# Last product in two token quarters with their own norms, conv pages from the common pool, residual updates two pages later

## The chip, the cores and the metric

The kernel runs on one core of one Trainium2 chip. The metric is the device time of one execution in microseconds (us); lower is better. A core has TensorE (matrix products; PE in the rows, its weight loads PEld), VectorE (DVE), ScalarE (ACT), GpSimd (POOL) and SyncE (SP), which here issues every DMA. TensorE writes into PSUM only; a PSUM bank holds 128x512 float32 values.

## What is computed

One layer of a hybrid backbone on 1024 latent tokens with 1024 channels, on a 16 x 64 grid: a modulated norm, a recurrent and a Fourier head group, an output projection with a gated residual; then the gated MLP with a 3x3 depthwise convolution, a gated residual and a last RMS norm. The change touches only the part from the convolution on:

```python
def conv_ffn(h, w_up, w_dw, b_dw, w_down, rows, cols):
    a, u = jnp.split(h @ w_up, 2, axis=-1)             # 1024 -> 2 x 2816
    a = depthwise_conv_3x3(a.reshape(B, rows, cols, D_FF), w_dw)
    a = a.reshape(B, L, D_FF) + b_dw
    return (jax.nn.gelu(a) * u) @ w_down               # 2816 -> 1024
...
h2 = modulate(rms_norm(x, norm2[l]), sh2, sc2)
x = x + gt2 * conv_ffn(h2, w_up[l], w_dw[l], b_dw[l], w_down[l], rows, GRID_W)
...
return rms_norm(x, norm_f)
```

## The kernel before

**Arithmetic.** All data are float32. For each product both operands are split into a high part (rounded, a copy on ScalarE, L62) and a low part (the rest, a subtraction on VectorE, L63); three TensorE products (high x high, high x low, low x high) are then summed in PSUM. Channels lie on the partitions and tokens along the free axis, so a tile is 128 channels x 512 tokens (one half of the tokens) or 128 x 1024 (a "page").

**MLP up (`norm2`, `ffn`, `product` L859, `plain` L74).** The 2816 hidden channels are 22 tiles `ff` of 128. The first two (`PLAIN`, ff 0 and 1) are computed by plain products, the other 20 by seven products of half size (a scheme of the Strassen kind, with sums U1 to U4 of blocks of the input as operands, made on VectorE at L808 to L819 in pages of the tag `cv`). For each ff the running sums are copied out of PSUM by ScalarE ("snap", L939) before TensorE goes on adding into the same bank.

**`gated`.** For each ff the gate branch `pa` lies in PSUM (tag `g`, two slots). ScalarE writes the centre tap and the bias into a page `cv` (L922); VectorE adds the eight other taps (L930); ScalarE applies the gelu (L932); VectorE multiplies by `u` (L933); then the page is stored to DRAM (`gd<-cv`). The tag `cv` has two slots, so a third page waits until the store of an earlier one has landed.

**MLP down (`down`).** The last product, 2816 to 1024, is done by seven products of half size again, q1, r5, r6, q3, q7, q2, q4 in this order, into the accumulators X (four banks of the tag `m`) and Z (two double banks of the tag `g`). A product has 6 "pages" p = 0 to 5; a page holds two blocks of 128 hidden channels, the last one a single block. For each page `prep` loads or adds up the weight side and the token side, `operands` splits both (L62, L63), and `step` (L1036) issues, for each of 4 output tiles j, three matmuls of 128 x 512 per block: 24 matmuls a page, 132 a product. The split pages come from three pairs of tags in turn (`wh`/`wl` twice, then `pg`; `ws`, `sh`/`sl`, `sh`/`sl`), each with two slots. The last two pages are held back and run tile by tile (`tail`), so that accumulator j is complete before j+1.

After each product `update` (L1067, VectorE) adds the accumulator times the gate to the residual x of one (token half, channel half); the first update of each loads x from DRAM (`pg<-x1d`). Token half 1 is complete after q7; `final` (L1158 on) norms, transposes and stores it inside q4, at its page 2, along with `squares` (sum of squares and transposes of x[0,0], L1107 to L1120). After q4 `update(0, 1, X)` and `last` finish token half 0: squares and norm gain (L1129, L1130), sums over channels by products with ones (L1135), 16 transposes (L1120), `rsqrt_mean` (L87 to L92), eight scalings out of PSUM on VectorE and ScalarE (L1147, L1149) and eight stores of 128 x 512.

**What sets the order.** A planner places the instructions: it steps through a model of the machine with modelled durations, and gives each engine the ready instruction that stands first in the program (blocks under `high_priority` go ahead). Slots of a tag are handed out in the same run. On the chip each engine then works through its own list strictly in order, and SP its DMAs too: what waits at the head holds up all behind it.

Of the kernel before, what the change touches and what calls it, by code (L numbers as in the profile page):

```python
# [34 lines left out]
class Kern:  # L35
# [389 lines left out]
    def hgrn(self, h, g):  # L425
# [60 lines left out]
        for d in range(2):  # L486
            s = st[d]
            f = g[d][0]
            c0, c1 = (0, 1) if d == 0 else (1, 0)
            A, Z = self.sm(16, f"A{d}"), self.sm(16, f"Z{d}")  # L490
            ZA, AZ = self.sm(8, f"ZA{d}"), self.sm(8, f"AZ{d}")
# [362 lines left out]
    def product(self, out, w, name, first):  # L854
        B = self.B[name]
        for kt in range(4):
            q, t = slice(kt * P, (kt + 1) * P), slice((kt % 2) * 512, (kt % 2 + 1) * 512)
            for j, (a, b) in enumerate(((0, 0), (0, 1), (1, 0))):
                self.nc.tensor.matmul(out, w[a][:, q], B[kt // 2][b][:, t], start=(first and kt == 0 and j == 0),  # L859
                                      stop=(kt == 3 and j == 2), skip_group_check=not first)  # L860
# [13 lines left out]
    def ffn(self):  # L874
# [9 lines left out]
        for ff in range(PLAIN, NF):  # L884
# [10 lines left out]
            with first():  # L895
                sv = snap(X)
            Z = self.pst("m")
            self.product(Z, w["S1"], "U1", True)
            with first():
                s5 = snap(Z)  # L900
            self.product(X, w["S3"], "U3", False)
# [15 lines left out]

    def gated(self, ff, pa, u):
        nc, V, v = self.nc, self.nc.vector, self.vec
        cv = self.pg(F32, "cv")  # L920
        w9 = lambda t: v[:, V_WDW + ff * 9 + t:V_WDW + ff * 9 + t + 1]
        nc.scalar.activation(cv, pa, AF.Identity, bias=v[:, V_BDW + ff:V_BDW + ff + 1], scale=w9(4))  # L922
        a3, c3 = pa.rearrange("p (r c) -> p r c", c=64), cv.rearrange("p (r c) -> p r c", c=64)
        for dr in (-1, 0, 1):
            for dc in (-1, 0, 1):
                if dr == 0 and dc == 0:
                    continue
                ro, co = slice(max(0, -dr), 16 - max(0, dr)), slice(max(0, -dc), 64 - max(0, dc))
                ri, ci = slice(max(0, dr), 16 + min(0, dr)), slice(max(0, dc), 64 + min(0, dc))
                V.scalar_tensor_tensor(c3[:, ro, co], a3[:, ri, ci], w9((dr + 1) * 3 + dc + 1), c3[:, ro, co],  # L930
                                       op0=MUL, op1=ADD)
        nc.scalar.activation(cv, cv, AF.Gelu_apprx_tanh)  # L932
        V.tensor_tensor(cv, cv, u, op=MUL)  # L933
        g = self.tile([P, 1024], F32, "gd")
        self.load(g, cv)
        self.gd.append(g)
# [6 lines left out]
    def down(self):  # L943
# [3 lines left out]
        nc, V, wd = self.nc, self.nc.vector, self.I["wd"]  # L947
        ng = self.sm(8, "ng2")
# [75 lines left out]
                out.append((hi, lo))  # L1024
            return out

        def product(pts, prep, first, then=None):

            n = (NF // 2 + 1) // 2

            def step(p, W, G, j):
                for i in range(num(p)):
                    w = slice(i * 512 + j * P, i * 512 + (j + 1) * P)
                    t = slice(i * 512, (i + 1) * 512)
                    for m, (a, b) in enumerate(((0, 0), (0, 1), (1, 0))):
                        nc.tensor.matmul(pts[j], W[a][:, w], G[b][:, t], start=first and p == 0 and i == 0 and m == 0,  # L1036
                                         stop=p == n - 1 and m == 2, skip_group_check=not first)

            tail = []
            for p in range(n):  # L1040
                if p == 2 and then:
                    then()
                W, G = operands(*prep(p), p)
                if p < n - 2:
                    for j in range(4):
                        step(p, W, G, j)
                else:
                    tail.append((p, W, G))
            for j in range(4):
                for t in tail:  # L1050
                    step(*t, j)

        x = {}

        def residual(half, r):
            x[half, r] = []
            for i in range(2):
                t = self.pg()
                self.load(t, self.x1d[half, 2 * r + i])
                x[half, r] += [t[:, :512], t[:, 512:]]  # L1060

        def update(half, r, pts):
            if (half, r) not in x:
                residual(half, r)
            for j in range(4):
                g = (ng if r else self.gt2)[:, 4 * r + j:4 * r + j + 1]
                V.scalar_tensor_tensor(x[half, r][j], pts[j], g, x[half, r][j], op0=MUL, op1=ADD)  # L1067

        def wide():
            pp = [self.pst("g"), self.pst("g")]  # L1070
            return [pp[i // 2][:, (i % 2) * 512:(i % 2 + 1) * 512] for i in range(4)]

        X = [self.pst("m") for _ in range(4)]
        product(X, q1, True)
        update(0, 0, X)
        Z = wide()
        product(Z, r5, True)
        update(1, 1, Z)
        product(X, r6, False)
        update(1, 0, X)  # L1080
        product(Z, q3, False)
        update(1, 0, Z)
        del Z
        product(X, q7, False)
        update(1, 1, X)
        Z = wide()
        product(Z, q2, True)
        update(0, 0, Z)
        del Z

        def then():
            residual(0, 1)
            self.final(x.pop((1, 0)) + x.pop((1, 1)))
            self.squares(x[0, 0])

        product(X, q4, False, then)
        update(0, 1, X)
        X.clear()
        self.last(x[0, 0], x[0, 1])

    def squares(self, xs):

        nc, V = self.nc, self.nc.vector
        self.acc = self.pg()
        for d, x in enumerate(xs):
            sq = self.acc[:, :512] if d == 0 else self.tile([P, 512], F32, "sn")
            nc.scalar.activation(sq, x, AF.Square)  # L1107
            if d:
                V.tensor_tensor(self.acc[:, :512], self.acc[:, :512], sq, op=ADD)
            nc.scalar.activation(x, x, AF.Copy, scale=self.vec[:, V_NF + d:V_NF + d + 1])  # L1110
        self.turn = []
        for i in range(4):
            if i % 2 == 0:
                pt = self.pst("g")
            self.turned(pt[:, (i % 2) * 512:(i % 2 + 1) * 512], xs, i)

    def turned(self, pt, xs, i):

        for j in range(4):
            self.nc.tensor.transpose(pt[:, j * P:(j + 1) * P], xs[j][:, i * P:(i + 1) * P], self.ident)  # L1120
        self.turn.append(pt)

    def last(self, xa, xb):

        nc, V = self.nc, self.nc.vector
        parts = [self.acc]
        for j, x in enumerate(xb):
            sq = self.tile([P, 512], F32, "sn")
            nc.scalar.activation(sq, x, AF.Square)  # L1129
            V.tensor_scalar(x, x, self.vec[:, V_NF + 4 + j:V_NF + 5 + j], None, op0=MUL)  # L1130
            parts.append(sq)
        ss = self.pst("m")
        for k, a in enumerate(parts):
            for i in range(4):
                nc.tensor.matmul(ss[:, i:i + 1], a[:, i * P:(i + 1) * P], self.ones[:, 0:1], start=(k == 0 and i == 0),  # L1135
                                 stop=k == 4, skip_group_check=True)
        for i in range(3):
            self.turned(self.pst("m"), xb, i)
        r = self.rsqrt_mean(ss[:, :4], 4, 1.0 / D, "nf")
        del ss  # L1140
        self.turned(self.pst("m"), xb, 3)
        for i in range(4):
            ob = self.pg()
            for h in range(2):
                o, pt = ob[:, h * 512:(h + 1) * 512], self.turn[4 * h + i]
                if h:
                    V.tensor_scalar(o, pt, r[:, i:i + 1], None, op0=MUL)  # L1147
                else:
                    nc.scalar.activation(o, pt, AF.Copy, scale=r[:, i:i + 1])  # L1149
                self.load(self.out[i, :, h * 512:(h + 1) * 512], o)  # L1150

    def final(self, xs):

# [47 lines left out]
NA, WARM, PLAIN = 3, 6, 2  # L1201
# [99 lines left out]
```

## Time and profile before

| | us |
|---|---|
| median of three runs | 1234.57 (1233.62 to 1239.16) |
| the profiled execution, device time | 1235.95 |
| its span, first to last instruction | 1234.2 |
| TensorE busy in the span | 1191.5 (97%) |
| VectorE busy | 913.7 (74%) |
| ScalarE busy | 559.3 (45%) |
| TensorE's mean granted clock | 0.987 of full speed |

Lines of a timeline begin with the start and the busy time in us; a bracket at the end is the engine's idle time just before and what ended it. The rows of a view by stage give busy time and instruction count of each engine, then the granted TensorE clock. Matmuls overlap in their pipeline, so the distance between two starts, not the busy time of one, is what a matmul costs.

### The profile page before, as it was taken

The page shows a single profiled execution, that of the slowest core. Times are in us where ns is not written, and L with a number is a line of the kernel's source. Part 1 is how long each engine was busy: PE and PEld are TensorE (multiplying, and loading weights), DVE is VectorE, ACT ScalarE, POOL GpSimd, SP SyncE. Part 2 cuts the span into 40 slices and gives each one's busy share as a digit, 9 for nine tenths or more (in the row PEclk, how much of TensorE's full clock was granted, in tenths as well). Part 3 has the DMA queues.
Part 4 walks back from the last instruction along what each step waited for, and adds up shares of the span by engine and source line. Part 5 has one row for each costly group of instructions (what it writes and reads, how often), then busy time and mean ns, then how long its engine had stood idle before and what let it go on. Part 6 is the DMA issues. An engine that isn't in the chain of part 4 may idle for free.

```text
span 1234.2 us, 15757 instructions
## 1 busy us (share of the span) xinstructions
PE 1191.5 (97%) x6120; PEld 996.5 (81%) x6120; DVE 913.7 (74%) x1173; ACT 559.3 (45%) x804; POOL 201.7 (16%) x124
## 2 busy tenths in 40 slices
PE   7999999999999999999989999999999999999997
PEld 4688888888998888888868888888888887887876
DVE  5761758585877457577989897888888888997683
ACT  5634545454431424364544444444354433335551
POOL 0000000000000000001336455364463400000000
PEclk9999999999999999999989999999999999999998
DMA  8631101010256037453122322222212438635642
GB/s 327 234 121 38 39 18 35 18 35 18 86 162 205 10 120 263 156 187 103 34 77 77 112 94 78 89 90 86 86 69 94 145 111 304 244 112 185 221 157 99
DMA packets 57867, 146.23 MB, mean 118 GB/s; under 512 B 5568, under 2 KB 5824, under 8 KB 57792
## 3 DMA queue, kind: packets, MB, share of 16 engines
q1 hardware_dynamic: 57792, 145.22, 34.1%
q8 instruction: 48, 0.79, 0.3%
q14 instruction: 27, 0.22, 0.1%
HBM read 125.27 MB, written 19.92 MB: 118 GB/s over the span
## 4 chain that ended last, share of the span: by engine, by line
PE 63%; DVE 14%; ACT 9%; DMA 8%; issue 5%; SPq 0%; POOL 0%; DVEq 0%; ACTq 0%; POOLq 0%
PE psm L859 27%; PE psm L74 16%; PE psg L74 14%; PE psm L1036 3%; DMA wr<-in_wd_dram 2%; DVE cv L930 2%; DVE wl L63 2%; DMA wm<-in_wm_dram 2%; DVE pg L451 1%; DMA pg<-gd 1%; ACT wh L62 1%; DMA wx<-gd 1%; ACT sq L568 1%; DVE sl L63 1%; PE psg L1036 1%
## 5 line engine op out<-in xcount | busy, mean ns | idle before, releaser
L930 DVE SCALAR_TENSOR_TENSOR cv<-psg,vec,cv 128x945 f32<-128x945 f32 (+2 forms) x176 | 213.8, 1219 | 26.9 <-ACT cv L922 23.1
L859 PE MATMUL psm<-pg,sh 128*128 128x512 f32 x640 | 199.1, 393 | 5.5 <-ACT sn L939 5.5
L62 ACT CAST wh<-wr 128x1024 fp32r<-128x1024 f32 x78 | 82.0, 1053 | 144.3 <-PE psg L74 39.7
L859 PEld LDWEIGHTS psm<-pg,sh 128*128 128x128 f32 x640 | 121.3, 190 | 31.6 <-ACT sn L939 6.3
L74 PE MATMUL psg<-pg,wh 128*128 128x512 f32 x472 | 134.8, 394 | 0.0
L63 DVE TENSOR_TENSOR wl<-wr,wh 128x1024 fp32r<-128x1024 f32 x78 | 96.5, 1238 | 41.2 <-ACT wh L62 40.8
L839 POOL TENSOR_TENSOR ws<-wx 128x512 f32<-128x512 f32 x20 | 27.9, 1394 | 601.8 <-DMA wx<-in_wup_dram 568.0
L859 PE MATMUL psm<-pg,sl 128*128 128x512 f32 x320 | 125.4, 392 | 0.0
L74 PEld LDWEIGHTS psg<-pg,wh 128*128 128x128 f32 x472 | 87.2, 188 | 16.8
L74 PE MATMUL psg<-wh,pg 128*128 128x256 f32 x512 | 99.0, 292 | 1.0 <-ACT wh L62 0.8
L859 PE MATMUL psm<-pg,wh 128*128 128x512 f32 x320 | 98.4, 389 | 0.0
L939 ACT ACTIVATE sn<-psm 128x512 f32<-128x512 f32 x80 | 47.6, 596 | 108.7 <-PE psm L859 108.7
L74 PEld LDWEIGHTS psg<-wh,pg 128*128 128x128 f32 x512 | 83.0, 197 | 1.6 <-ACT wh L62 1.4
L74 PE MATMUL psg<-pg,wl 128*128 128x512 f32 x236 | 79.1, 395 | 0.0
L74 PE MATMUL psg<-wl,pg 128*128 128x256 f32 x256 | 74.5, 292 | 4.6 <-DVE wl L63 4.6
L859 PEld LDWEIGHTS psm<-pg,sl 128*128 128x128 f32 x320 | 60.6, 190 | 12.7
L859 PEld LDWEIGHTS psm<-pg,wh 128*128 128x128 f32 x320 | 60.1, 188 | 12.4
L905 POOL TENSOR_TENSOR uu<-sn,sn 128x512 f32<-128x512 f32 x20 | 38.5, 1924 | 183.0 <-ACT sn L939 183.0
L859 PE MATMUL psm<-pg,wl 128*128 128x512 f32 x160 | 62.2, 389 | 0.0
L74 PE MATMUL psm<-pg,pg 128*128 128x128 f32 (+2 forms) x256 | 56.6, 348 | 5.0 <-DVE pg L506 4.7
L221 DVE SCALAR_TENSOR_TENSOR ma<-wm,silu_c,ma 128x512 f32<-128x512 f32 x56 | 41.9, 749 | 17.8 <-DMA wm<-in_wm_dram 17.2
L847 POOL TENSOR_TENSOR sl<-ws,sh 128x1024 fp32r<-128x1024 f32 x20 | 54.1, 2706 | 5.6 <-ACT sh L846 5.5
(368 smaller groups left out, 2590.3 us busy)
## 6 DMA issues: line engine op xcount, KB each, us to landing
wr<-in_wd_dram SPq DMA_DIRECT2D x35, 512.0 KB, 3.7
wm<-in_wm_dram SPq DMA_DIRECT2D x64, 256.0 KB, 3.0
wx<-in_wup_dram SPq DMA_DIRECT2D x22, 512.0 KB, 4.5
wr<-in_wup_dram SPq DMA_DIRECT2D x22, 512.0 KB, 3.6
gd<-cv SPq DMA_DIRECT2D x22, 512.0 KB, 2.6
pg<-gd SPq DMA_DIRECT2D x33, 256.0 KB, 4.9
ld<-in_wm_dram SPq DMA_DIRECT2D x16, 512.0 KB, 7.9
wr<-in_wo_dram SPq DMA_DIRECT2D x16, 512.0 KB, 3.6
```

What stands on the lines that cost most here:

```text
L62: self.nc.scalar.copy(hi, raw)
L63: self.nc.vector.tensor_tensor(lo, raw, hi.bitcast(F32), op=SUB)
L74: self.nc.tensor.matmul(out, lhsT, rhs, start=start, stop=stop)
L221: nc.vector.scalar_tensor_tensor(acc, w, s, acc, op0=MUL, op1=ADD)
L451: V.tensor_tensor_scan(flip(lf, d), flip(lf, d), self.mscan, 0.0, op0=ADD, op1=MUL)
L839: G.tensor_tensor(s31[:, hi], u[:, lo], u[:, hi], op=ADD)
L847: G.tensor_tensor(S31[1], s31, S31[0].bitcast(F32), op=SUB)
L859: self.nc.tensor.matmul(out, w[a][:, q], B[kt // 2][b][:, t], start=(first and kt == 0 and j == 0), stop=(kt == 3 and j == 2), skip_group_ ...
L905: self.nc.gpsimd.tensor_tensor(u[:, h1], s7, s5, op=SUB)
L930: V.scalar_tensor_tensor(c3[:, ro, co], a3[:, ri, ci], w9((dr + 1) * 3 + dc + 1), c3[:, ro, co], op0=MUL, op1=ADD)
L939: self.nc.scalar.mul(dst, src, c)
L1036: nc.tensor.matmul(pts[j], W[a][:, w], G[b][:, t], start=first and p == 0 and i == 0 and m == 0, stop=p == n - 1 and m == 2, skip_group_ch ...
```

## The change

1. **Conv pages.** In `gated` the page of ff 0 and 1 comes from the common pool `pg` (33 pages) in place of the tag `cv`.
2. **Residual updates.** The `update` of a product no longer stands behind it, but inside the next product, ahead of its page 2 (`then`), along with the load of x where it is the first. The order of the products and their accumulators stays; the second use of Z is called Y.
3. **Last product.** In q4 the last three pages are held back, not two. They run first for tokens 0 to 255 of the half (all four j), then for tokens 256 to 511: 120 matmuls of 256 columns in place of 60 of 512. Behind each quarter stands its own `quarter`: update of 128 x 256, squares, sums with ones, `rsqrt_mean` of two columns, scaling, stores. The 16 transposes of x[0,0] move from `squares` into the quarters (the second quarter's eight are put ahead of its update).

```diff
     def gated(self, ff, pa, u):
-        cv = self.pg(F32, "cv")
+        cv = self.pg(F32, "pg" if ff < PLAIN else "cv")
...
-        def product(pts, prep, first, then=None):
+        def product(pts, prep, first, then=None, half=None):
...
-            def step(p, W, G, j):
+            def step(p, W, G, j, q):
...
-                        nc.tensor.matmul(pts[j], W[a][:, w], G[b][:, t], start=first and p == 0 and i == 0 and m == 0,
+                        nc.tensor.matmul(pts[j][:, q], W[a][:, w], G[b][:, i * 512 + q.start:i * 512 + q.stop],
+                                         start=first and p == 0 and i == 0 and m == 0,
...
-                if p < n - 2:
+                if p < n - (3 if half else 2):
...
-            for j in range(4):
-                for t in tail:
-                    step(*t, j)
+            for q in (slice(0, 256), slice(256, 512)) if half else (slice(0, 512),):
+                for j in range(4):
+                    for t in tail:
+                        step(*t, j, q)
+                if half:
+                    half(q)
...
-        product(X, q1, True)
-        update(0, 0, X)
-        Z = wide()
-        product(Z, r5, True)
-        update(1, 1, Z)
-        product(X, r6, False)
...
+        Z = wide()
+        product(Z, r5, True, lambda: update(0, 0, X))
+        product(X, r6, False, lambda: update(1, 1, Z))
+        product(Z, q3, False, lambda: update(1, 0, X))
...
+        product(X, q7, False, free_z)
+        Y = wide()
+        product(Y, q2, True, lambda: update(1, 1, X))
...
+        product(X, q4, False, norm, lambda q: self.quarter(q, X, ng, x[0, 0], x[0, 1]))
...
+    def quarter(self, q, X, ng, xa, xb):
+        last = q.start > 0
+        ts = [slice(q.start + i * P, q.start + (i + 1) * P) for i in range(2)]
+        if last:
+            pa = self.pst("g")
+            for i in range(2):
+                self.turned(pa[:, i * 512:(i + 1) * 512], xa, ts[i])
+        acc = self.acc[:, q]
+        for j in range(4):
+            x = xb[j][:, q]
+            V.scalar_tensor_tensor(x, X[j][:, q], ng[:, 4 + j:5 + j], x, op0=MUL, op1=ADD)
+            sq = self.tile([P, 512], F32, "sn")[:, :256]
+            nc.scalar.activation(sq, x, AF.Square)
+            if j < 3:
+                V.tensor_tensor(acc, acc, sq, op=ADD)
+            V.tensor_scalar(x, x, self.vec[:, V_NF + 4 + j:V_NF + 5 + j], None, op0=MUL)
...
+        for k, a in enumerate((acc, sq)):
+            for i in range(2):
+                nc.tensor.matmul(ss[:, i:i + 1], a[:, i * P:(i + 1) * P], self.ones[:, 0:1], start=(k == 0 and i == 0),
...
+        r = self.rsqrt_mean(ss, 2, 1.0 / D, "nf")
...
+            for h in range(2):
+                o = ob[:, h * 512:(h + 1) * 512]
+                if i:
+                    V.tensor_scalar(o, pts[h], r[:, i:i + 1], None, op0=MUL)
...
+                self.load(self.out[q.start // P + i, :, h * 512:(h + 1) * 512], o)
```

## Rows read from the trace of the kernel before

**Rows 1.** Busy time by stage: us, then PE, PEld, DVE, ACT, POOL (instructions), granted clock, DMA
```profile
600.00:620.00 20.00, 20.00 (x90) 16.57 (x89) 19.82 (x16) 10.37 (x12) 8.41 (x5) 1.00 0.09 27
...
640.00:660.00 20.00, 18.87 (x70) 15.07 (x71) 18.00 (x15) 8.46 (x12) 9.68 (x6) 0.84 0.19 56
...
700.00:800.00 100.00, 100.00 (x441) 82.30 (x440) 83.09 (x74) 45.31 (x58) 49.33 (x30) 1.00 0.25 91
```
**Rows 2.** TensorE's waits at the lines of the MLP's products: us in total, times, longest
```profile
PE psm L859 <- ACT sn L939: 5.5, 2, 5.1
...
PE psm L1036 <- DVE sl L63: 2.9, 2, 1.9
...
PE psg L1036 <- DVE sl L63: 1.0, 1, 1.0
...
PE psg L1036 <- DVE ws L63: 0.3, 1, 0.3
```
**Rows 3.** Timeline of SP and ScalarE around the longest wait
```profile
632.92 0.38 SPq L59 DMA_DIRECT2D gd<-cv  x1
...
638.97 1.20 ACT L922 ACTIVATE cv<-psg,vec 128x1024 f32<-128x1024 f32 x1 [4.67 <-DMA gd<-cv]
640.07 1.08 ACT L939 ACTIVATE sn<-psm 128x512 f32<-128x512 f32 x2
```
**Rows 4.** Timeline of TensorE behind that wait
```profile
640.71 1.22 PE L859 MATMUL psm<-pg,sh 128*128 128x512 f32 x2 [5.07 <-ACT sn L939]
...
646.81 0.61 PE L859 MATMUL psm<-pg,sh 128*128 128x512 f32 x2
```
**Rows 5.** Timeline of VectorE at the start of q4
```profile
1183.18 1.40 DVE L1067 SCALAR_TENSOR_TENSOR pg<-psg,gt,pg 128x512 f32<-128x512 f32 x2
...
1185.63 1.22 DVE L63 TENSOR_TENSOR sl<-pg,sh 128x1024 fp32r<-128x1024 f32 x1
```
**Rows 6.** Residual loads: by group (KB, us to landing), then one pair and its reader
```profile
pg<-x1d SPq DMA_DIRECT2D x8, 512.0 KB, 5.2
...
1045.48 0.87 SPq L59 DMA_DIRECT2D pg<-x1d  x2
...
1055.12 1.40 DVE L1067 SCALAR_TENSOR_TENSOR pg<-psg,ng,pg 128x512 f32<-128x512 f32 x2
```
**Rows 7.** Matmul starts at 256 and 512 columns, and the loads (min/median/max ns)
```profile
116.87 0.28 PE L74 MATMUL psc<-pg,wl 128*128 128x256 f32 x1
...
117.23 0.28 PE L74 MATMUL psc<-pg,wl 128*128 128x256 f32 x1
...
1217.84 0.39 PE L1036 MATMUL psm<-sl,pg 128*128 128x512 f32 x1
...
1218.07 0.39 PE L1036 MATMUL psm<-sh,pg 128*128 128x512 f32 x1
...
L74 PEld LDWEIGHTS psc<-pg,wh x128: 187/192/192, 115.3 to 313.0; 128*128 128x128 f32 x128
```
**Rows 8.** Timeline inside q4: ScalarE behind a store, transposes of `squares`
```profile
1201.46 0.69 ACT L1176 ACTIVATE uu<-psg,n2r 128x512 f32<-128x512 f32 x1 [1.87 <-DMA out_dram<-uu]
...
1204.29 1.91 PE L1120 MATMUL psg<-ident,pg 128*128 128x128 f32 x16
```
**Rows 9.** Timeline behind the last matmul, and the last stores (first and last start)
```profile
1218.30 0.94 PE L1135 MATMUL psm<-ones,pg 128*128 128x1 f32 x8
...
1218.49 0.75 DVE L1067 SCALAR_TENSOR_TENSOR pg<-psm,ng,pg 128x512 f32<-128x512 f32 x1
...
1219.28 0.63 ACT L1129 ACTIVATE sn<-pg 128x512 f32<-128x512 f32 x1 [1.41 <-DVE pg L1067]
...
1224.26 0.16 DVE L87 TENSOR_SCALAR nfs<-psm 128x4 f32<-128x4 f32 x1 [3.83 <-PE psm L1135]
...
1225.57 2.73 DVE L1147 TENSOR_SCALAR pg<-psm,nfr 128x512 f32<-128x512 f32 x4
...
L59 SPq DMA_DIRECT2D out_dram<-pg x8: 332/468/602, 1226.3 to 1230.1; - x8
```

More of the change, by code (lines that the diff above doesn't have):

```diff
@@ L1025, in operands @@
             return out
-        def product(pts, prep, first, then=None):
+        def product(pts, prep, first, then=None, half=None):
             n = (NF // 2 + 1) // 2
-            def step(p, W, G, j):
+            def step(p, W, G, j, q):
                 for i in range(num(p)):
                     w = slice(i * 512 + j * P, i * 512 + (j + 1) * P)
-                    t = slice(i * 512, (i + 1) * 512)
                     for m, (a, b) in enumerate(((0, 0), (0, 1), (1, 0))):
-                        nc.tensor.matmul(pts[j], W[a][:, w], G[b][:, t], start=first and p == 0 and i == 0 and m == 0,
+                        nc.tensor.matmul(pts[j][:, q], W[a][:, w], G[b][:, i * 512 + q.start:i * 512 + q.stop],
+                                         start=first and p == 0 and i == 0 and m == 0,
                                          stop=p == n - 1 and m == 2, skip_group_check=not first)
@@ L1043, in product @@
                 W, G = operands(*prep(p), p)
-                if p < n - 2:
+                if p < n - (3 if half else 2):
                     for j in range(4):
-                        step(p, W, G, j)
+                        step(p, W, G, j, slice(0, 512))
                 else:
                     tail.append((p, W, G))
-            for j in range(4):
-                for t in tail:
-                    step(*t, j)
+            for q in (slice(0, 256), slice(256, 512)) if half else (slice(0, 512),):
[4 more added lines that the diff above has]
+                    half(q)
         x = {}
@@ L1074, in down, with free_z, norm @@
         product(X, q1, True)
-        update(0, 0, X)
         Z = wide()
-        product(Z, r5, True)
-        update(1, 1, Z)
-        product(X, r6, False)
[L1080 to L1085, printed above, removed]
-        Z = wide()
[L1087 to L1091, printed above, removed]
+        product(Z, r5, True, lambda: update(0, 0, X))
+        product(X, r6, False, lambda: update(1, 1, Z))
+        product(Z, q3, False, lambda: update(1, 0, X))
+        def free_z():
+            update(1, 0, Z)
+            Z.clear()
+        product(X, q7, False, free_z)
+        Y = wide()
+        product(Y, q2, True, lambda: update(1, 1, X))
+        def norm():
+            update(0, 0, Y)
+            Y.clear()
             residual(0, 1)
@@ L1094, in then @@
             self.squares(x[0, 0])
[L1096 to L1099, printed above, removed]
+        product(X, q4, False, norm, lambda q: self.quarter(q, X, ng, x[0, 0], x[0, 1]))
     def squares(self, xs):
@@ L1110, in squares @@
             nc.scalar.activation(x, x, AF.Copy, scale=self.vec[:, V_NF + d:V_NF + d + 1])
-        self.turn = []
-        for i in range(4):
-            if i % 2 == 0:
-                pt = self.pst("g")
[L1115 to L1143, printed above, removed]
@@ new lines, in turned @@
+    def turned(self, pt, xs, t):
+        for j in range(4):
+            self.nc.tensor.transpose(pt[:, j * P:(j + 1) * P], xs[j][:, t], self.ident)
+    def quarter(self, q, X, ng, xa, xb):
+        nc, V = self.nc, self.nc.vector
+        last = q.start > 0
[5 more added lines that the diff above has]
+        acc = self.acc[:, q]
+        for j in range(4):
+            x = xb[j][:, q]
[5 more added lines that the diff above has]
+            V.tensor_scalar(x, x, self.vec[:, V_NF + 4 + j:V_NF + 5 + j], None, op0=MUL)
+        if last:
+            X.clear()
+        ss = self.pst("g")[:, :2]
+        for k, a in enumerate((acc, sq)):
+            for i in range(2):
+                nc.tensor.matmul(ss[:, i:i + 1], a[:, i * P:(i + 1) * P], self.ones[:, 0:1], start=(k == 0 and i == 0),
+                                 stop=k == 1, skip_group_check=True)
+        if last:
+            pb = [self.pst("m") for _ in range(2)]
+            for i in range(2):
+                self.turned(pb[i], xb, ts[i])
+        r = self.rsqrt_mean(ss, 2, 1.0 / D, "nf")
+        del ss
+        for i in range(2):
+            ob = self.pg()
+            if last:
+                pts = pa[:, i * 512:(i + 1) * 512], pb[i]
+            else:
+                pt = self.pst("g")
+                pts = pt[:, :512], pt[:, 512:]
+                for p, xs in zip(pts, (xa, xb)):
+                    self.turned(p, xs, ts[i])
@@ L1144, in last @@
             for h in range(2):
-                o, pt = ob[:, h * 512:(h + 1) * 512], self.turn[4 * h + i]
-                if h:
-                    V.tensor_scalar(o, pt, r[:, i:i + 1], None, op0=MUL)
-                else:
-                    nc.scalar.activation(o, pt, AF.Copy, scale=r[:, i:i + 1])
-                self.load(self.out[i, :, h * 512:(h + 1) * 512], o)
+                o = ob[:, h * 512:(h + 1) * 512]
+                if i:
+                    V.tensor_scalar(o, pts[h], r[:, i:i + 1], None, op0=MUL)
+                else:
+                    nc.scalar.activation(o, pts[h], AF.Copy, scale=r[:, i:i + 1])
```

## The prediction

> **What bounds the kernel now.** I read the busy time by stage first, then TensorE's waits, then the timeline at each wait and behind the last matmul. The stages say that from the MLP on TensorE is the bound: 100 of 100 us busy in a steady stretch, with VectorE second at 83% [rows 1]. So time can only come from three places: the moments at which TensorE stands still, the work that it does without need, and the stretch after its last matmul. The waits are few [rows 2]: 5.5 us in two waits at the products of `ffn` (5.1 us in one), 4.2 us in four at those of `down`. From the last matmul of q4 (start 1218.07, end about 1218.46 [rows 7]) to the end of the span at 1234.2 there are 15.7 us.
>
> **The change, part 1: conv pages.** The long wait ends at 640.71 [rows 4]. The reader follows it back: TensorE waited for a copy out of PSUM (L939) that ran at 640.07, right behind L922, which stood at the head of ScalarE's list until 638.97 and waited for a DMA, the store of a conv page that SP issued only at 632.92 [rows 3]. That is the first conv page of ff 2, with no free `cv` slot since ff 0 and 1 hold both until their stores land. With the pages of ff 0 and 1 in the common pool, ff 2 finds a `cv` slot that was free long before, and L922 no longer waits there. Gone are 5.07 us of standing still, and what comes behind: the stage 640 to 660 has a granted clock of 0.84, that is, part of it at 1.2 GHz in place of 2.4. Fifteen matmuls start between 640.71 and 646.81, 6.10 us [rows 4]; at the warm distance of 0.23 us [rows 7] they take 3.4. So 2.7 us more, 7.8 in all. What is late next? ff 3 then waits for nothing that ff 2 held, and ff 4 for ff 2's store, as every later ff in the steady stretch, where TensorE doesn't wait. VectorE was full just before in the stage 600 to 620 [rows 1] and the same taps only move forward into its idle time. Cost of the edit: two common pages. No row shows how many are free at 605 us. If the page of ff 0 comes late, its taps start late and the PSUM slot that ff 2 needs is late: from 0 (VectorE is full anyway) up to the whole 7.8 us lost. I take 0, since the operands that fill the pool are written by then, and keep the other end as a rival.
>
> **Part 2: updates two pages later.** All four waits in `down`, 2.9 + 1.0 + 0.3 us [rows 2], end with a split on VectorE (`sl` or `ws`, L63) at the first pages of a product. At the last of them VectorE ran two updates (L1067, 1.40 us) from 1183.18, and the split that TensorE waited for came at 1185.63 [rows 5]. With the updates behind the preparation of pages 0 and 1 that split comes 1.4 to 2.8 us earlier (four updates are 2.8), more than the wait of 1.9. VectorE's total is the same, so the same 2.8 us now stand ahead of page 2, which has a page (24 matmuls at 0.23, 5.4 us) more cover; part of the wait may reappear there. Gain between 0 and 4.2; I take 3.0, nearer to the whole, because the waits are shorter than what is moved. The residual loads move too. SP issues them behind the loads of two more pages; before, one pair was issued at 1045.48 and read at 1055.12, 9.6 us later, against 5.2 us to landing [rows 6]. Both ends move by two pages, so the cover stays about 4 us. An accumulator is read two pages into a product on the other one, so no matmul waits for it.
>
> **Part 3: two quarters.** Costs inside TensorE's stream, all before its last matmul. (a) 120 matmuls of 256 columns for 60 of 512: three of 256 start within 0.36 us, so 0.12 each, 14.4 us; 60 at 0.227 are 13.6. Cost 0.8. (b) Of 32 transposes, 24 now stand ahead of the last matmul, not 16: 16 take about 1.66 us of the stream [rows 8], so eight cost 0.8. (c) The first quarter's sums: eight instructions, as the eight that took 0.94 [rows 9]: 0.9. (d) A new wait. Page 5 is now needed after two steps (12 matmuls of 256, 1.4 us) where it had all of page 3 as cover, and its token side needs a slot that page 2 releases; its split waits behind scalings that wait for a store, 1.87 us in one case [rows 8]. Between 0 and 1.9; the planner can put other tiles first, so I take 0.5. Queued behind that wait on TensorE is everything to the end. Sum 3.0 to 3.1.
>
> Gain behind the last matmul. Before: update, square (0.75 and 0.63), then sums until the norm chain starts at 1224.26, 5.8 us after the last matmul; scalings from 1225.57, 1.3 later; the last of eight stores starts at 1230.1 and the span ends 4.1 us after it [rows 9]. After, for 256 columns: update about 0.45 and square about 0.4 (estimates, between half and the whole of those rows), four sum instructions for the last square and the waits between, in all 1.75; chain 1.25; the first scaling 0.7. Then four stores at the old distance (seven steps in 3.8 us, 0.55 each): the last starts at 3.7 + 1.65 = 5.4 and the end is 4.1 later, at 9.5. The first quarter's chain (sums, scalings, four stores) takes about 7 us from its end and lies beside the second quarter's 7.2 us of matmuls. Saved 15.7 − 9.5 = 6.2; with the cost of 3.1 a net 3.1, bounds 1.5 (wait of 1.9, estimates high) to 4.5.
>
> A rule speaks against (a). The rows show a weight load of 0.19 us and matmuls of 256 columns that start every 0.12, so loads run beside earlier matmuls and loads. The Trainium skill, "TensorE: Matmul & The Clock Gate", section "Part 3: Packing small matmuls", says that a load overlaps a running matmul only when it goes to other rows of the array; here each load fills all rows. By that rule a matmul of 256 could not start closer than its load lasts; the price is worked out as a rival below. The trace disagrees.
>
> **Sum.** 1234.2 − 7.8 − 3.0 − 3.1 = 1220.3; with the 1.75 us around the span 1222.05. The profiled execution lies 1.4 us above the median of the runs, so on the median's footing 1220.7: **1221**.
>
> **Rivals.**
> - *The stall moves.* VectorE was full until 635 and the pool nearly so; if the page or the PSUM slot comes late, TensorE waits elsewhere in 600 to 660. For: no free time on VectorE there. Against: TensorE itself had no wait before 635. From half to all of 7.8, and up to 2 more: 1225 to 1231.
> - *Slower: residual loads late.* The load of x stands behind page loads that wait for slots; VectorE reaches the update and stands still, with all later splits queued behind. It decides once the load is issued less than 5.2 us before the update. At three products (r5, r6, q3) up to 5.2 us less 1 to 2 of cover, about 4, and behind a wait of that size the 2.7 us at the lower clock: 3 x 6.7 = 20, and part 2's gain is lost: 1238 to 1244. Against: 9.6 us of lead before.
> - *Page 5 late,* gain of part 3 gone: 1224 to 1226.
> - *Part 2 does nothing,* because the planner, which orders by readiness, had the updates late already or puts them back: 1224. Against: the rows show updates ahead of the late split.
> - *Weight loads pace the halves:* 0.19 x 120 = 22.8 in place of 14.4, 8.4 more: 1229.4.
>
> **How the numbers follow.** Forecast 0.55 (own range 1217 to 1225), the stall moves 0.20 (half of it above 1228.4), residual loads 0.07, page 5 0.09, part 2 nothing 0.06, weight loads 0.03. A measurement of this kernel can tell about 0.5%, 6.2 us, from no change, so faster means below 1228.4: 0.55 + 0.10 + 0.09 + 0.06 = 0.80; within 0.10 + 0.03 = 0.13; slower 0.07. The range 1216.5 to 1229.5 leaves out the slower case, the upper part of the moved stall and the ends of the forecast.
>
> **What would show it.** Part 1: no wait for L939 near 640 and a granted clock of 1.00 in 640 to 660. Part 2: no waits for `sl` at the second pages of r5, q7, q4, and no VectorE wait for the x loads. Part 3: matmuls of 256 columns at 0.12, the last one ending near 1234.2 − 15.7 − 7.8 − 3.0 + 3.1 = 1210.8, only four stores after it, and 9 to 10 us from there to the end of the span. Wrong would be a wait of over 2 us in 600 to 660, or at page 5 of q4.

## The result, and the profile after

The changed kernel takes 1222.76 us (median of 4 runs, 1221.22 to 1224.47) beside 1234.66 us for the kernel before in the same series (4 runs): a ratio of 0.9897 [0.9869, 0.9925]. In two later series, each on one chip, it took 1224.98 (6 runs; ratio 0.9932 [0.9909, 0.9955]) and 1227.24 us (6 runs; 0.9925 [0.9908, 0.9941]). The gain is thus 8 to 13 us, clear of noise; 13.6 had been forecast. But it did not come from where the forecast put it, as the traces show.

The span of the profiled executions in four stretches, worked out from the starts of the lines named: cut at the first half-size product of the MLP (first start at L859), the first and the last matmul start of the `down` products (L1036 before, L1035 after), and the end:

| us | before | after | difference |
|---|---|---|---|
| start to first L859 | 605.6 | 600.2 | −5.4 |
| L859 to first `down` product | 390.9 | 388.4 | −2.5 |
| `down`, first to last matmul start | 221.6 | 221.7 | +0.1 |
| last matmul start to end of span | 16.1 | 9.2 | −6.9 |
| span | 1234.2 | 1219.4 | −14.7 |

The first row can't be the change: up to the convolution's first page (L922), which is written at about the first half-size product, the instructions of each engine are the same, and in the same order. Busy time by stage shows where those 5.4 us are: us, then PE, PEld, DVE, ACT, POOL (instructions), granted clock, DMA share, GB/s. Before:

```profile
0.00:20.00 20.00, 13.39 (x62) 7.03 (x62) 10.99 (x31) 12.53 (x19) 0.20 (x4) 0.91 0.85 301
20.00:40.00 20.00, 18.16 (x94) 12.17 (x94) 12.85 (x22) 10.46 (x18) 0.00 (x0) 0.91 1.00 386
380.00:400.00 20.00, 18.00 (x137) 17.80 (x138) 15.11 (x20) 3.06 (x4) 0.00 (x0) 0.91 0.63 220
440.00:460.00 20.00, 18.24 (x141) 18.23 (x141) 13.14 (x31) 2.24 (x3) 0.00 (x0) 0.91 0.41 132
```

The same stretches after, and then the stages around the place that part 1 was to mend [rows 1]:

```profile
0.00:20.00 20.00, 14.67 (x70) 7.14 (x70) 12.13 (x35) 13.65 (x21) 0.20 (x4) 1.00 0.86 321
20.00:40.00 20.00, 16.80 (x109) 11.39 (x112) 12.29 (x22) 9.93 (x16) 0.00 (x0) 1.00 0.97 374
380.00:400.00 20.00, 18.22 (x153) 18.02 (x152) 17.14 (x23) 3.06 (x4) 0.00 (x0) 1.00 0.56 198
440.00:460.00 20.00, 20.00 (x169) 20.00 (x168) 9.09 (x24) 1.54 (x2) 0.00 (x0) 1.00 0.35 121
...
620.00:640.00 20.00, 17.20 (x76) 13.94 (x75) 19.56 (x19) 10.18 (x13) 8.05 (x6) 1.00 0.30 119
640.00:660.00 20.00, 20.00 (x90) 16.54 (x89) 19.79 (x18) 9.66 (x13) 10.55 (x7) 1.00 0.29 93
```

In four stretches that the change doesn't touch, the execution of before had TensorE at 1.2 GHz for part of the time (0.91), and the execution of after never had. The lead of after grows in just these: to 2.7 us by 55 us, to 4.0 by 415 and to 5.4 by 470. So the span of one execution can't tell a difference of under 5 us; from here on a part is judged by the stage that it acts in, and by medians.

In the MLP's first stage the wait of 5.07 us [rows 2, 4] is gone, but 620 to 640 is no longer full. TensorE's waits after, at the lines of the MLP's products (us in total, times, longest):

```profile
PE psm L859 <- DVE psg L893: 2.8, 1, 2.8
PE psm L859 <- ACT sn L939: 2.4, 3, 1.5
PE psg L1183 <- DVE n2s L87: 0.9, 1, 0.9
PE psm L1035 <- DVE sl L63: 0.6, 1, 0.6
PE psg L1035 <- DVE sl L63: 0.4, 2, 0.2
PE psm L1035 <- DVE ws L63: 0.3, 1, 0.3
PE psg L1183 <- ACT uu L1188: 0.2, 1, 0.2
```

Waiting at L859 fell from 5.5 us to 5.2: a new wait of 2.8 us for VectorE's L893, which writes the PSUM slot `g` of ff 2, and 2.4 us in three where 0.4 had been left. At `down` the four waits of 4.2 us became 2.4 us in six, 1.1 of them at L1183, the transposes of `final`, whose norm now comes later.

The timeline behind the last matmul of q4, to be held against [rows 7, 9]:

```profile
1200.59 0.50 PE L1139 MATMUL psg<-ones,pg 128*128 128x1 f32 x4
1200.96 0.96 PE L1114 MATMUL psg<-ident,pg 128*128 128x128 f32 x7
...
1202.80 1.14 PE L1114 MATMUL psg<-ident,pg 128*128 128x128 f32 x9
...
1210.12 0.28 PE L1035 MATMUL psm<-sl,pg 128*128 128x256 f32 x1
...
1210.24 0.28 PE L1035 MATMUL psm<-sh,pg 128*128 128x256 f32 x1
1210.36 1.04 PE L1114 MATMUL psg<-ident,pg 128*128 128x128 f32 x8
...
1210.56 0.48 DVE L1128 SCALAR_TENSOR_TENSOR pg<-psm,ng,pg 128x256 f32<-128x256 f32 x1
1211.14 0.42 ACT L1130 ACTIVATE sn<-pg 128x256 f32<-128x256 f32 x1 [1.38 <-DVE pg L1128]
1211.24 0.50 PE L1139 MATMUL psg<-ones,pg 128*128 128x1 f32 x4
...
1211.74 0.50 PE L1139 MATMUL psg<-ones,sn 128*128 128x1 f32 x4
...
1212.29 0.16 DVE L87 TENSOR_SCALAR nfs<-psg 128x2 f32<-128x2 f32 x1 [0.34 <-PE psg L1139]
...
1213.57 0.69 ACT L1161 ACTIVATE pg<-psg,nfr 128x512 f32<-128x512 f32 x1 [0.88 <-DVE nfr L92]
...
1214.28 1.90 SPq L59 DMA_DIRECT2D out_dram<-pg  x4
```

Matmuls of 256 columns start 0.12 us apart to the last; from its start the norm chain begins 2.05 us later (6.2 before, 1218.07 to 1224.26), four stores go out where eight did, and the span ends after 9.2 us. Of the 32 transposes of the outputs, 16 stand ahead of the last matmul, as before; the planner put the eight of the second quarter's first tiles (1210.36) behind it, beside the update and the square.

### The profile page after: what moved, and what is told of

The parts are those of the page before. It is cut to its first block, busy times and chain, and to the rows that moved or that the text cites. A ratio compares the mean times of both kernels' runs of the same rounds, so it can differ in the third digit from the quotient of the medians.

```text
span 1219.4 us, 15862 instructions
## 1 busy us (share of the span) xinstructions
PE 1181.7 (97%) x6156; PEld 989.0 (81%) x6156; DVE 917.8 (75%) x1192; ACT 560.2 (46%) x809; POOL 201.9 (17%) x124
## 4 chain that ended last, share of the span: by engine, by line
PE 62%; DVE 18%; ACT 9%; DMA 5%; issue 5%; SPq 0%; DVEq 0%; ACTq 0%
PE psm L859 24%; PE psm L74 16%; PE psg L74 13%; PE psm L1035 4%; DVE cv L930 4%; PE psg L1035 3%; DVE wl L63 2%; DMA wm<-in_wm_dram 2%; DVE pg L451 1%; DVE pg L930 1%; DVE sl L63 1%; ACT sq L568 1%; ACT L444 1%; ACT L445 1%; DMA ld<-in_wm_dram 1%
## 5 line engine op out<-in xcount | busy, mean ns | idle before, releaser
L930 DVE SCALAR_TENSOR_TENSOR cv<-psg,vec,cv 128x945 f32<-128x945 f32 (+2 forms) x160 | 195.2, 1220 | 24.0 <-ACT cv L922 20.4
L859 PE MATMUL psm<-pg,sh 128*128 128x512 f32 x640 | 197.1, 389 | 0.6 <-ACT sn L939 0.6
L859 PEld LDWEIGHTS psm<-pg,sh 128*128 128x128 f32 x640 | 120.0, 188 | 25.9 <-ACT sn L939 1.1
L859 PE MATMUL psm<-pg,sl 128*128 128x512 f32 x320 | 124.5, 389 | 0.0
L859 PE MATMUL psm<-pg,wh 128*128 128x512 f32 x320 | 98.6, 389 | 2.8 <-DVE psg L893 2.8
L939 ACT ACTIVATE sn<-psm 128x512 f32<-128x512 f32 x80 | 47.7, 597 | 109.6 <-PE psm L859 109.6
L74 PE MATMUL psg<-wh,pg 128*128 128x256 f32 x512 | 96.4, 287 | 0.9 <-ACT wh L62 0.8
L859 PEld LDWEIGHTS psm<-pg,wh 128*128 128x128 f32 x320 | 60.0, 188 | 15.6 <-DVE psg L893 3.2
L859 PEld LDWEIGHTS psm<-pg,sl 128*128 128x128 f32 x320 | 60.1, 188 | 12.5
L859 PE MATMUL psm<-pg,wl 128*128 128x512 f32 x160 | 62.3, 389 | 0.0
```

Of the source, the lines that this page charges most:

```text
L74: self.nc.tensor.matmul(out, lhsT, rhs, start=start, stop=stop)
L939: self.nc.scalar.mul(dst, src, c)
```

## The experiments

**One part alone, and both others.** The three parts were put one by one on the kernel before, and parts 2 and 3 together. All four ran on one chip, with 19 runs of the kernel before (median 1235.08).

```diff
 # p1_conv_pages: before, and
-        cv = self.pg(F32, "cv")
+        cv = self.pg(F32, "pg" if ff < PLAIN else "cv")
 # p2_updates: before, and
-        update(0, 0, X)
-        product(Z, r5, True)
+        product(Z, r5, True, lambda: update(0, 0, X))
... (the other updates likewise)
 # p3_quarters: before, with `product`, `step`, `squares` and `quarter` of after, and
-        product(X, q4, False, then)
-        update(0, 1, X)
-        X.clear()
-        self.last(x[0, 0], x[0, 1])
+        product(X, q4, False, then, lambda q: self.quarter(q, X, ng, x[0, 0], x[0, 1]))
 # p23_no_conv_pages: after, and
-        cv = self.pg(F32, "pg" if ff < PLAIN else "cv")
+        cv = self.pg(F32, "cv")
```

> Part 1 alone on the kernel before. The stage from the first matmul of the half-size up products (L859) to the first of the down products took 390.8 us before and 388.4 after the whole change, not the 383 that the prediction stands on. Theory: the common pool has no free page until the plain products release the four pages of the block B12, so the centre taps of ff 0 and ff 1 start together and late, both PSUM slots stay taken, and a wait of 2 to 3 us for the sum of ff 2 (L893) replaces most of the stall; the stage is 388 to 389, the whole 1232. Rival: that wait belongs to the one execution profiled after, in which TensorE came to the MLP 5.4 us earlier; then the stage is near 383 and the whole 1227.

> Part 2 alone on the kernel before: updates and residual loads two pages later, the last product as before. Theory: the waits for sl and ws at the first pages of the down products fall from 4.2 us to about 1.3, the down stage (first to last down matmul) from 221.7 to 218.5 to 219, the whole 1231.5. Rival, the residual loads arrive late: waits of VectorE for the x loads of several us and a stage above 222. Rival, the planner had ordered so before: 221.7.

> Part 3 alone on the kernel before: the last product in two quarters, updates and conv pages as before. Theory: the down stage grows by 2.5 to 3 (120 matmuls of 256 columns 0.8, eight more transposes 0.8, eight sum instructions 0.9, page 5 up to 0.5) to 224.5, the stretch behind the start of the last matmul falls from 16.1 to about 9.3, the whole 1230.5. Rival, page 5 comes late: a wait of over 1.5 us in the first quarter and a stage of 226 or more.

> The changed kernel without part 1 (conv pages from their own two slots). Theory: the stall of 5 us for the store and the lower clock behind it are back (stage 390.8), all else as after: 1225, 2.4 above the changed kernel. Rival, part 1 is worth its full 7.8: 1230.

| | us, median | ratio to before | L859 stage | `down` | end |
|---|---|---|---|---|---|
| before (stages of its one profile) | 1235.08 | | 390.9 | 221.6 | 16.1 |
| part 1 alone | 1232.67 | 0.9988 [0.9977, 0.9999] | 390.0 | 221.8 | 15.6 |
| part 2 alone | 1232.74 | 0.9979 [0.9965, 0.9993] | 389.0 | 221.0 | 16.1 |
| part 3 alone | 1228.77 | 0.9950 [0.9935, 0.9965] | 391.1 | 223.7 | 9.2 |
| parts 2 and 3 | 1226.45 | 0.9927 [0.9911, 0.9944] | 389.2 | 221.4 | 9.2 |

By the ratios part 1 gives 1.5 us (0.1 to 2.8 by the interval; 2.4 by the medians), part 2 2.6 (0.9 to 4.3) and part 3 6.2 (4.3 to 8.0), in all 10.3. Part 1 alone has the same new wait as after, 2.8 us for L893, and in its execution the granted clock behind it was 0.91 in 620 to 640. TensorE's waits from the first `down` product on, with part 2 alone:

```profile
PE psm L1036 <- DVE ws L63: 1.8, 1, 1.8
...
PE psg L1170 <- DVE n2s L87: 0.9, 1, 0.9
```

Part 2 alone removes the four waits of 4.2 us and makes two of 2.7: one for `ws` at the start of r6 (1054.12) and one at the norm of `final`. Its stage gains 0.6 us on the old last product, where 2.7 to 3.2 had been expected, and 2.3 where part 3 is there (223.7 to 221.4). One execution is a weak measure here: in the nine profiled executions that have parts 2 and 3 the stage is 220.7 to 222.9, so 0.8 to 3.0 below that of part 3 alone. Part 3 costs 2.1 us in the stream and gains 6.9 behind it. Its stage (223.7) lies below the expected 224.5, that of part 1 (390.0) above the expected 388 to 389.

**Which page comes late.** Why does part 1 leave a stall of half the length? Rows from the timelines of ScalarE and VectorE at the start of the convolutions, before:

```profile
605.44 1.22 ACT L922 ACTIVATE cv<-psg,vec 128x1024 f32<-128x1024 f32 x1 [3.34 <-DVE pg L772]
...
609.05 1.21 ACT L922 ACTIVATE cv<-psg,vec 128x1024 f32<-128x1024 f32 x1
...
606.68 1.20 DVE L930 SCALAR_TENSOR_TENSOR cv<-psg,vec,cv 128x945 f32<-128x945 f32 x1
...
625.28 0.68 DVE L893 TENSOR_TENSOR psg<-sn,psm 128x512 f32<-128x512 f32 x1
```

and after:

```profile
601.21 1.05 ACT L771 CAST pg<-cv 128x1024 fp32r<-128x1024 f32 x1 [4.48 <-DVE cv L819]
602.16 1.04 ACT L846 CAST sh<-ws 128x1024 fp32r<-128x1024 f32 x1
603.11 0.58 ACT L803 COPY uu<-psm 128x512 f32<-128x512 f32 x1
603.59 2.31 ACT L922 ACTIVATE pg<-psg,vec 128x1024 f32<-128x1024 f32 x2
...
604.83 4.56 DVE L930 SCALAR_TENSOR_TENSOR pg<-psg,vec,pg 128x945 f32<-128x945 f32 x4 [1.32 <-ACT pg L922]
...
625.11 0.68 DVE L893 TENSOR_TENSOR psg<-sn,psm 128x512 f32<-128x512 f32 x1
```

Counted from the first L859 matmul (605.6 and 600.2), the writing of the page of ff 0 (L922) began 0.1 us ahead of it before and 3.4 behind it after, right ahead of that of ff 1; the first tap came 1.1 us behind it before and 4.6 after, with VectorE idle for 1.32. The taps of both tiles then interleave, so neither lets go of its slot `g` early: fifteen taps (L930) run ahead of L893 of ff 2 where thirteen did, and L893 comes 24.9 us behind the first L859 matmul instead of 19.7. The next four runs, on one chip, tell whether it is the page of ff 0 that is late, or both, or the pool as such. The kernel before ran 11 times there (median 1233.32).

```diff
 # again: after, unchanged.  The others, each on after:
-        cv = self.pg(F32, "pg" if ff < PLAIN else "cv")
+        cv = self.pg(F32, "pg" if ff == 0 else "cv")                    # ff0_from_pool
+        cv = self.pg(F32, "pg" if ff == 1 else "cv")                    # ff1_from_pool
+        cv = self.pg(F32, "pg" if PLAIN <= ff < PLAIN + 2 else "cv")    # ff2_ff3_from_pool
```

> The changed kernel once more, beside the variants on the same chip. The order of the instructions up to the first conv page is that of the kernel before, so what differs ahead of the MLP is scatter: the first matmul of the MLP (L859) began at 600.2 to 605.6 us in six profiled executions. Expected: that start between 600 and 606, the MLP stage (first L859 to first down matmul) 388 to 390, with a wait of 2.8 for L893 and one of 1.5 for L939; the whole 1221 to 1226.

> The changed kernel with only the page of ff 0 from the common pool, ff 1 in its own slot. Theory (the pool has no page until the plain products are through, so a page from there starts late): ff 1 now starts first and ff 0 late, both hold their PSUM slots as long as after, and the wait for L893 stays at 2 to 3 us, the stage 388 to 390. Rival (two pages that start together and share VectorE are the cause, not the late page): the wait falls below 1 us and the stage to 385 or less.

> The changed kernel with only the page of ff 1 from the common pool; ff 0 stays in its own slot, and the other slot is free for ff 2. Theory: the centre tap of ff 0 comes before the plain products end, as before, its PSUM slot is free in time for ff 2 and the wait for L893 goes to below 0.5; ff 2 doesn't wait for a store either. MLP stage 383 to 385, the whole 4 to 5 us below the changed kernel. Rival (the sum of VectorE's work up to there is the bound, whatever its order): a wait of 2 to 3 us stays somewhere in 620 to 690, stage 387 to 389.

> The changed kernel with the pages of ff 2 and ff 3 from the common pool, when it has room, and ff 0 and ff 1 in their own slots, so that the order up to there is that of before. Theory: no wait for the store, none for L893, MLP stage 383 to 385, the whole 4 to 5 us below the changed kernel and near ff 1 from the pool. Rival as there: 387 to 389.

| pages from the pool | us, median | ratio to before | L859 stage | wait for L893 | other waits at L859 |
|---|---|---|---|---|---|
| ff 0 and 1 (`again`) | 1224.98 | 0.9932 [0.9909, 0.9955] | 390.1 | 2.8 | 2.4 |
| ff 0 | 1222.64 | 0.9909 [0.9884, 0.9933] | 386.2 | 1.6 | 1.8 |
| ff 1 | 1222.74 | 0.9908 [0.9884, 0.9932] | 385.9 | 0 | 3.4 |
| ff 2 and 3 | 1221.03 | 0.9891 [0.9865, 0.9917] | 386.1 | 0 | 3.3 |

ScalarE's first pages with ff 0 from the pool (first L859 matmul at 603.7), and under it with ff 1 from the pool (also 603.7):

```profile
603.60 1.21 ACT L922 ACTIVATE cv<-psg,vec 128x1024 f32<-128x1024 f32 x1 [3.39 <-PE psm L74]
...
607.06 1.22 ACT L922 ACTIVATE pg<-psg,vec 128x1024 f32<-128x1024 f32 x1
```

```profile
603.62 1.21 ACT L922 ACTIVATE cv<-psg,vec 128x1024 f32<-128x1024 f32 x1 [3.33 <-DVE pg L772]
...
607.13 1.21 ACT L922 ACTIVATE pg<-psg,vec 128x1024 f32<-128x1024 f32 x1
```

Whichever of the two tiles has the pool page is written 3.4 us behind the first L859 matmul, the one with its own buffer 0.1 ahead of it. For ff 1 that is no delay: its turn is then in the kernel before too (609.05, 3.5 behind 605.6). For ff 0 it is: ff 1 convolves first, and TensorE still waits 1.6 us for L893. So the late page is shown, and its harm is to ff 0.

The timelines split this harm in two. With ff 0 alone from the pool VectorE starts its taps on time (1.2 us behind the first L859 matmul, on ff 1), but fifteen run ahead of L893, as after, and it comes at 22.7; only with both pages from the pool is the first tap late as well, and L893 comes at 24.9. With ff 1, or ff 2 and 3, from the pool thirteen taps run ahead of it, and it comes at 19.4 and 19.7, as before. So neither side of the expectation for ff 0 held: it missed the theory's 2 to 3 us and the rival's below 1.

On the chip the late page did not wait for its slot: ScalarE ran without idle time from 601.21 into L922, which stood behind L771, L846 and L803 in its list. Why the planner put it there, and whether the slot was free much sooner, no row shows.

The sizes were expected too large: with the stall and L893's wait both gone, the stage is 385.9 to 386.1 and not 383 to 385, because new waits for L939 appear. The last of them with ff 2 and 3 from the pool, and what held up ScalarE ahead of it:

```profile
698.65 1.06 ACT L932 ACTIVATE cv<-cv 128x1024 f32<-128x1024 f32 x1 [4.37 <-DVE cv L930]
...
701.19 0.73 PE L859 MATMUL psm<-pg,ah 128*128 128x512 f32 x2 [2.17 <-ACT sn L939]
```

The copy L939 (at 700.54) stands in ScalarE's list behind a gelu (L932) that waited 4.37 us for VectorE's taps. VectorE is nearly full ahead of it (19.8 to 19.9 of 20 us in each stage from 600 to 660), so what it owes by then is paid further on.

**Four of them side by side.** The variants of the last table lie close together, so the best, after, parts 2 and 3, and the best variant's pages on the kernel before were run once more on one chip, with 11 runs of before (1235.79).

```diff
 # before_ff23: before, and
-        cv = self.pg(F32, "cv")
+        cv = self.pg(F32, "pg" if PLAIN <= ff < PLAIN + 2 else "cv")
```

> The changed kernel again, as the measure for the other three on the same chip. Theory (part 1 only moved the stall of before: the two plain tiles' convolutions now interleave and keep both PSUM slots g): 388 to 390 us from the first half-size product to the first down product, with the wait of 2.8 us for L893 in it; 1223 to 1225 us. Rival (the place of the pages makes no difference, and the earlier differences of 2 to 4 us between the variants are scatter of executions): the same time as all other kernels here that have parts 2 and 3.

> The changed kernel without part 1: all pages of the convolution from their own two buffers, as in the kernel before, with parts 2 and 3. Theory: 389 to 390 us to the first down product with the wait of 5 us in it, and 1 us or less above the changed kernel, so 1224 to 1226 us. Rival (part 1 brings what its stall suggested): 4 us or more above the changed kernel.

> The changed kernel, with only the pages of the two tiles behind the plain ones (ff 2 and ff 3) from the common pool. Theory: the plain tiles convolve one after the other as in the kernel before, and the wait for a page's store is gone too: no wait for L893, about 386 us to the first down product, and 2 to 4 us below the changed kernel, 1220 to 1222 us. Rival: within 1 us of it.

> The kernel before, with only the pages of ff 2 and ff 3 from the common pool, and neither part 2 nor part 3. Theory: the stage to the first down product falls from 390.8 to about 386 us, nothing else moves, and the time falls by 4 to 5 us, to 1230 us, where part 1 as it was made gave 1 to 2. Rival (the gain of these pages hangs on the later parts): 1232 to 1233 us, as part 1 alone.

| | us, median | ratio to before | L859 stage |
|---|---|---|---|
| after (`after_5`) | 1227.24 | 0.9925 [0.9908, 0.9941] | 389.8 |
| parts 2 and 3 (`p23_5`) | 1225.72 | 0.9923 [0.9905, 0.9942] | 389.2 |
| parts 2 and 3, ff 2 and 3 from the pool (`ff23_5`) | 1221.34 | 0.9878 [0.9860, 0.9897] | 386.1 |
| before, ff 2 and 3 from the pool (`before_ff23`) | 1231.18 | 0.9955 [0.9939, 0.9972] | 387.8 |

Beside parts 2 and 3, part 1 as it was made brings nothing that these runs can tell (1227.24 against 1225.72). After lies above its expected 1223 to 1225. The same edit for the two tiles behind the plain ones takes 4.4 us off (1225.72 to 1221.34), and 0.45% or 5.6 us off the kernel before; by the medians 4.6. That version is below both kernels. The waits at L859 in `before_ff23`:

```profile
PE psm L859 <- ACT sn L939: 3.4, 2, 2.2
```

Its stage is 1.7 us longer than in `ff23_5` with the same waits. In 700 to 720, behind the wait of 2.2 us, its granted clock was 0.91; in `ff23_5` it was 1.00.

## Why the prediction was right, and where it was not

Forecast were 1221 us, by way of −7.8, −3.0 and −3.1; measured was 1222.8, and 1225.0 and 1227.2 in the later series. The time came out near the forecast, but the mechanism in the MLP was the rival's. By the runs of one part alone, part 1 gave 1.5 in place of 7.8, part 2 2.6 in place of 3.0, and part 3 6.2 in place of 3.1: two errors in opposite directions, of which the second makes up for half of the first. That the first series came within 2 us is luck.

**Part 1: the step "I take 0" for a late page of ff 0 failed.** The prediction named the mechanism (a late page, late taps, a late PSUM slot for ff 2) and its other end, and kept it as "the stall moves"; that is what happened. What made it choose 0 was that VectorE is full anyway and that the pool's operands are written by then. Neither was reason enough: ScalarE comes to the pool page only 3.4 us behind the first L859 matmul (that a page which is written is not yet free, since the plain products still read it, would be a cause, but is not shown), and VectorE stood idle for 1.32 us waiting for L922 before the taps became the bound. The prediction's own sign of being wrong, a wait of over 2 us in 600 to 660, is there: 2.8 us for L893. Its two signs of being right, no wait for L939 near 640 and a clock of 1.00 in 640 to 660, came true as well, so they could not tell the stall that went from the stall that moved. Of the 7.8 us, 1.5 came by the runs of part 1 alone, and none that can be told beside parts 2 and 3. The rival's time of 1225 to 1231 holds the 1227.2 of the third series and all but holds the 1225.0 of the second; the first lies below it.

The other half of the step was mis-sized too: the variants in which ff 0 has its own page gain 4.8 to 5.0 us in the stage (390.9 to 386.1 and 385.9), not 7.8. The sum closes: waits of 5.5 become 3.4, and the 2.7 us at the lower clock go, 4.8. What was missing is an answer to "What is late next?": the text looked at ff 3 and ff 4, not at VectorE's backlog, which comes due at 679 and 700.

The 2.7 us for the clock stood on one execution. The granted clock behind the 5 us stall was below 1.00 in all five kernels here that had it, so the term was real, but not always of that size. Less its waits at L859, the stage lasts 382.5 to 383.2 us in the five executions whose clock stayed at 1.00 in it; with the 5 us stall it lasts 385.4 before and 385.7 with part 3 alone, but 383.9 to 384.1 in the other three. Behind the new wait of 2.8 us the clock was 0.91 in three executions of four as well, and the stage less its waits lasted 384.6 to 384.9 in these three: the new stall costs more than its length, and that takes back most of what part 1 removes.

**Part 2: inside its bounds, below its value in most stages.** 3.0 were forecast (0 to 4.2). The runs of part 2 alone give 2.6 (0.9 to 4.3), which cannot tell 3.0 from 1; the stage gives 0.6 alone and 0.8 to 3.0 beside part 3. So part of the waiting reappears, but not at page 2, where the text put it. It is at `ws` of the next product (1.8 us, part 2 alone) and at `final`'s norm (0.8 to 1.0 us, in every kernel with part 2), a place that the prediction did not price, though the diff moves `final` with the updates. VectorE's splits at q4, after (sl, the updates behind it, and the matmul that waited):

```profile
1175.20 1.22 DVE L63 TENSOR_TENSOR sl<-pg,sh 128x1024 fp32r<-128x1024 f32 x1
1176.34 1.40 DVE L1070 SCALAR_TENSOR_TENSOR pg<-psg,gt,pg 128x512 f32<-128x512 f32 x2
1176.47 0.50 PE L1035 MATMUL psm<-sl,wh 128*128 128x512 f32 x1 [0.56 <-DVE sl L63]
```

In [rows 5] the updates stood ahead of the split and TensorE waited 1.9 us; now they stand behind it, and it waits 0.56. That rules out the rival by which the planner leaves the updates where they were. In the ten executions with part 2 this wait is from none to 1.7 us (`ff23_5`), so the move does not always remove it.

**Part 3: the mechanism was right, the cost was set too high.** The tail was forecast at 9.5 us from the last matmul's end; it is 8.9 from there (9.2 from its start), a gain of 6.9 between the starts instead of 6.2. In the stream the four terms were 0.8, 0.8, 0.9 and 0.5; the trace of part 3 alone shows 2.1. Of these (a) holds: 0.12 us for each matmul of 256 columns, 0.8 in all. (c) is 0.74: eight matmuls of one column, in two groups of four, each of which puts off what follows by 0.37 us (1200.59 to 1200.96 above). (b) is nothing: the planner placed eight of the transposes behind the last matmul, where the text counted them ahead of it. (d) is nothing: page 5's split is done before its first use, as the trace of after shows, which names no wait there:

```profile
1193.37 0.69 DVE L63 TENSOR_TENSOR sl<-pg,sh 128x512 fp32r<-128x512 f32 x1 [1.04 <-ACT sh L62]
...
1194.83 0.28 PE L1035 MATMUL psm<-sh,pg 128*128 128x256 f32 x1
```

The rest, 0.6, is a `ws` wait of 0.9 in place of 0.3 [rows 2], which no term held and which is 0.3 again after. By the stages part 3 thus nets 4.8 where 3.1 was forecast; the 6.2 of its runs has an interval of 4.3 to 8.0, which holds the 4.8.

**The rivals.** Residual loads late: no. They are issued as far ahead as before, and land later, but in time: no wait of VectorE for them is named in the trace of after. The group (KB, us to landing), and one pair with its reader, 9.4 us behind:

```profile
pg<-x1d SPq DMA_DIRECT2D x8, 512.0 KB, 7.2
...
1040.07 1.59 SPq L59 DMA_DIRECT2D pg<-x1d  x2
...
1049.43 1.40 DVE L1070 SCALAR_TENSOR_TENSOR pg<-psg,ng,pg 128x512 f32<-128x512 f32 x2
```

The cover by the group's landing fell from 4.4 us (9.6 less 5.2) to 2.2. Page 5 late: no, by the row at 1194.83. Weight loads as the pace: no; the loads take 0.19 us after too, and the matmuls of 256 columns start 0.12 apart. The Trainium skill ("TensorE: Matmul & The Clock Gate", "Part 3: Packing small matmuls") states that a weight load overlaps a running matmul only when it goes to other rows of the array. The trace of after contradicts that for loads of all 128 rows, as that of before did.

**The footing.** The sum was made against an execution with four slow stretches ahead of the MLP, 5.4 us that no part owns, and the text took off only 1.4 for it, the distance to the median. That the profiled span after, 1219.4, lies so near the forecast 1220.3 is an accident of this: −5.4 that nobody forecast stands for the 5.3 that the MLP stage failed to give (−2.5 in the place of −7.8).

## What to carry to other kernels

A buffer moved to a shared pool has a date as well as a place: ask when the new user gets its turn in its engine's list against the moment at which it is due, and give the pool's slot to a user whose turn comes late anyway; here the same edit was worth little or nothing for the first two tiles and 4 to 6 us for the two behind them. When a stall goes, price what the busiest other engine (here VectorE at 19.8 of 20 us) owes by then, since that backlog is the next wait. Compare two single executions stage by stage, and first look at a stage that the change can't have touched.

## What the runs showed of the hardware that was not expected

The same wait of 2.8 us, at the same place in the same stream, was followed by a granted clock of 1.00 in one execution of the changed kernel (620 to 640, above) and by 0.91 in two others, as here in `after_5`:

```profile
620.00:640.00 20.00, 17.20 (x70) 13.78 (x69) 18.27 (x19) 10.29 (x12) 9.08 (x6) 0.91 0.31 108
```

TensorE was busy for the same 17.20 us with six instructions fewer started. And in every profiled kernel here but `after`, some of the stretches 0 to 40, 380 to 400 and 420 to 460 had a granted clock below 1.00, though none of the kernels differs there; the first half-size product started between 600.2 us (no such stretch) and 605.6 (before, with four; `after_5`, with the stretches at 20, 380, 420 and 440). By and large the start came later the more time an execution spent at the lower clock ahead of it. What decides that from one execution to the next stayed open.
